# Moving part of the last scan quarter's matrix work ahead of the scan's end, and summing later output weights by DMA

## The chip, the cores and the metric

The kernel runs on one core of one Trainium2 chip, as one program. The metric is the device time of one execution in microseconds, the median over several executions. The core's engines are named as in the profile: PE (matrix multiplications, into PSUM), PEld (loading of PE's weights), DVE, ACT and POOL (elementwise work), and SP, which here only starts transfers. ACT and POOL can start transfers too; POOL's can add into their target ("accumulate").

## The reference, cut to what matters

One layer of a diffusion backbone: a bidirectional S5 mixer on 1024 latent and 256 context tokens, then a SwiGLU feed-forward network, both behind RMS norms with scale and shift. The work that the change touches is the S5 mixer:

```python
def run(u, h0):                                   # once per direction, 64 groups x 64 complex states
    bu = jnp.einsum('lgh,gnh->lgn', u, b_bar)
    bu = bu.at[0].add(lam_bar * h0)
    a = jnp.broadcast_to(lam_bar, bu.shape)
    _, h = lax.associative_scan(_linear_combine, (a, bu), axis=0)
    return jnp.einsum('lgn,ghn->lgh', h, c_mat).real, h[-1]
y = y_forward + reversed(y_backward) + d_skip * h
g = jax.nn.gelu(y);  out = g * jax.nn.sigmoid(g @ w_glu + b_glu)
```

## The kernel before, in words

The 1024 latent tokens are cut into 128 blocks of 8. Inside a block the output is a multiplication with a small lag (Toeplitz) matrix; between blocks, states are carried by a scan over 128 block positions. The 64 groups of channels are handled as four **quarters** q = 0..3, each of two **eighths** k = 2q, 2q+1. For each eighth the output is the sum of an input part (`x_mm`, L945: 16 matrix multiplications with the Toeplitz tiles) and a state part (`states_mm`, L922: the states times the quarter's output weights `CL[q]`). The state part is done in two halves, an early one over block positions whose states are there before the scan ends, and a late one; the direction that runs backwards is read through a turned copy of the states (`turned`, L902 and L904).

The scan itself (`scan`, L839 to L864) runs on DVE alone, from 128.7 to 228.57 us. It restores the odd block positions of some quarters as it goes; for others `fill` restores them on POOL, from the even ones. Everything else near it is written out by hand, in two strings of tokens: `PROG1` (L32) lists what the other engines do while the scan runs, `PROG2` (L33, L34) what follows, and `run` executes a string token by token, so a token's place fixes the order of its instructions on every engine and queue that it uses. The digit behind the letter is the eighth (for C: quarter and part, for F: quarter and half).

The tokens that matter here:

- **Cqp** (`cl_ops`, L659): part p of quarter q's output weights: two products of 128x1024 on POOL (L77) and their sum. `HOWS` (L30) says how each sum is made: P by four PE multiplications with the identity (L672) and two ACT copies (L673), E by a POOL addition (L77), Y by a transfer started by POOL that adds into its target (L675).
- **Kk** (`k_mats`): the lag matrices of an eighth: 32 + 8 + 32 PE instructions (L809, L813, L817) into two PSUM tiles that were zeroed before (`zeros`, L771, two of ACT's copies, or DVE's memset, L966), then two ACT copies (L821), each followed by a transfer to `kd` in DRAM that ACT starts (L822). **Tu** reads that back as a Toeplitz tile (SP, L830).
- **Pk**: `x_mm` and the early half of `states_mm`; **Yj**: ACT copies one of its two PSUM tiles to SBUF (L997). **Rk** turns the early states (ACT). **Nk**: the late half; **Zk** turns the late states; **Dk** adds late to early (DVE); **Hk** is the gelu (ACT).
- **Qk** (k = 6, 7 only): `x_mm` and both halves at once (`states_all`, L935), after the scan, with the gelu read from PSUM (L1009). The lag matrices K6 and K7 stand after the scan too, and so do T12 to T15.
- **I, J** transpose the result (L1056) for the gate's multiplication **g** (`glu_mm`, L1097 to L1099), which starts at 267.49 us; **w, l** load its weights, **W, V** split them for the matrix unit. After it comes the feed-forward network, to the end.

Of the kernel before, what the change touches and what calls it, by code (L numbers as in the profile page):

```python
# [42 lines left out]
def s5_ffn_kernel(tc, a, out):  # L43
# [3 lines left out]
    with ctx:  # L47
# [611 lines left out]
        def cl_ops(q, part, ct, how):  # L659
# [7 lines left out]
            def add():  # L667
# [8 lines left out]
                else:  # L676
# [18 lines left out]
        cts = [[ct_[0], ct_[0], ct_[1], ct_[2]], [ct_[0], ct_[1], ct_[2], ct_[0]], [ct_[1], ct_[2], ct_[0], ct_[1]], [ct_[3], ct_[0]] * 2]  # L695
        CL0 = cl_ops(0, 0, cts[0][0], SY) + cl_ops(0, 1, cts[0][1], SY)
        CLAT = {12: 1, 13: 1, 14: 2}
        for hb in range(16):
# [210 lines left out]
        def yview(k, gp):  # L909
            return Y[:, k].rearrange("p t (a e h) -> p e a t h", e=2, h=HC)[:, gp]  # L910

        def states_mm(k, pts, half, hs, start):

            for a_ in range(4):
                for ri in range(2):
                    for d in range(2):
                        cs_ = slice(64 * (half ^ d), 64 * (half ^ d) + 64)
                        c0 = 31 + 64 * half
                        for gp in range(2):
                            ps = slice(64 * gp, 64 * gp + 64)  # L920
                            st = hs[ps, :, ri, a_] if d else STQ[k // 2][ps, c0:c0 + 64, ri, 8 * (k % 2) + a_]
                            PE.matmul(flat(pts[gp][cs_, a_]), st, flat(CL[k // 2][ps, ri, d, 4 * (k % 2) + a_]),  # L922
                                      start=start and ri == 0, stop=ri == 1 and (start or a_ == 3))

        def states_all(k, pts, hs):

            for a_ in range(4):
                for ri in range(2):
                    for d in range(2):
                        for c in range(2):  # L930
                            cs_ = slice(64 * c, 64 * c + 64)
                            for gp in range(2):
                                ps = slice(64 * gp, 64 * gp + 64)
                                st = hs[ps, cs_, ri, a_] if d else STQ[k // 2][ps, 31 + 64 * c:95 + 64 * c, ri, 8 * (k % 2) + a_]
                                PE.matmul(flat(pts[gp][cs_, a_]), st, flat(CL[k // 2][ps, ri, d, 4 * (k % 2) + a_]),  # L935
                                          start=False, stop=a_ + ri + d == 5)
# [10 lines left out]

        scan()
        inner = {}
        HSe = [view(r, kb, [64, 2, 4]) for r, kb in ((RC[3], 14), (RC[3], 12), (RC[3], 14), (RC[3], 12), (RA, 2), (RA, 0))]  # L950
        HSl = [view(RA, STB * (i // 3) + 4.125 + 2 * (i % 3), [64, 2, 4]) for i in range(6)]
        HSq = {6: view(RA, 0, [P, 2, 4]), 7: view(RA, STB, [P, 2, 4])}

        def run(prog):


            for w in prog.split():
# [2 lines left out]
                    ada(i)  # L960
                elif op == "M":
                    mod_cols(i)
                elif op == "k":
                    KT[i] = [pe8([15 * HC]) for _ in range(2)]
                    for kv in KT[i]:
                        V.memset(kv, 0.0)  # L966
                elif op == "K":
                    k_mats(*divmod(i, 2), KT.get(i) or [kt, zeros(pw([15 * HC])) if i < 4 else pm[:, 0:15 * HC]])
                elif op == "L":
                    cs_load(i, S)  # L970
                elif op == "G":
                    cs_sign(i)
                elif op == "B":
                    bb_put(1, bb_turn(1))
                    bb_put(0, bb_turn(0))
                elif op == "C":
                    q, part = divmod(i, 10)
                    for f in cl_ops(q, part, cts[q][part], HOW[q][part]):
                        f()
                elif op == "F":  # L980
                    fill(*divmod(i, 10), *((RW, 0) if i >= 30 else (RC[3], 12)))
                elif op == "T":
                    toeplitz(i)
                elif op == "R":
                    turned(i, 0, HSe[i], S)
                elif op == "Z":
                    turned(i, 1, HSl[i], ENG[ZEN[i]])
                elif op == "z":
                    turned(i, 2, HSq[i], ENG[ZEN[i]])
                elif op == "P":  # L990
                    inner[i] = x_mm(i, pw)
                    states_mm(i, inner[i], 0, HSe[i], False)
                elif op == "Q":
                    inner[i] = x_mm(i, pe8)
                    states_all(i, inner[i], HSq[i])
                elif op == "Y":
                    S.copy(yview(i // 2, i % 2), inner[i // 2][i % 2])  # L997
                elif op == "N":
                    late[i] = [pe8([4, T, HC]) for _ in range(2)]
                    states_mm(i, late[i], 1, HSl[i], True)  # L1000
                elif op == "D":
                    for gp, po in enumerate(late[i]):
                        tt(yview(i, gp), po, yview(i, gp), ADD)
                elif op == "H":
                    if i in late:
                        S.activation(Y[:, i], Y[:, i], AF.Gelu_apprx_tanh)
                    else:
                        for gp in range(2):
                            S.activation(yview(i, gp), inner[i][gp], AF.Gelu_apprx_tanh)  # L1009
# [31 lines left out]
        KT = {}  # L1041
# [731 lines left out]
```

## Time and profile before

| what | us |
| --- | --- |
| median of 3 runs (lowest, highest) | 1023.78 (1023.33, 1025.45) |
| span of the profiled execution, first to last instruction | 1022.5 |
| scan on DVE | 128.7 to 228.57 |
| first late half (N0) on PE | 228.72 |
| first matrix multiplication of the gate | 267.49 |
| PE busy, of 25 us from 225 / from 275 | 18.78 / 25.00 |

The profiled execution has no time of its own beside its span; the median of the runs lies 1.3 us above that span, which is the time around the first and the last instruction. In rows of the timeline the first number is the start in us, the second how long the group took from its first start to its last end; what stands in brackets is how long the engine sat idle before it, and which instruction it waited for. In the rows by window, "PEclk" is the clock that PE was granted, 1.00 being full speed.

### The profile page before, as it was taken

What the parts mean: (1) busy time and instruction counts of PE and PEld (TensorE: products, weight loads), DVE (VectorE), ACT (ScalarE), POOL (GpSimd) and SP (SyncE); (2) the same over time, 40 slices, a digit from 0 to 9 for tenths busy, and PEclk for the clock granted to TensorE, in tenths of its full rate; (3) what the DMA queues carried; (4) which work ended last, traced back from release to release, by engine and by line L of the source; (5) the groups of instructions that cost most, each with busy time, mean ns of one, the idle gap of its engine ahead of it and who ended that gap; (6) DMA issues with size and microseconds to landing.
All of it is one profiled execution on the core that took longest, in us unless ns stands there. A gap on an engine that the chain in (4) does not pass through costs nothing. (4 is left out here: it accounts for less than half of the span.)

```text
span 1022.5 us, 18552 instructions
## 1 busy us (share of the span) xinstructions
PE 962.6 (94%) x6988; PEld 774.2 (76%) x6988; DVE 785.6 (77%) x1642; ACT 438.5 (43%) x858; POOL 762.7 (75%) x590
## 2 busy tenths in 40 slices
PE   5987798868999999999999999999999999999996
PEld 1466523658999988778888888888888888888885
DVE  7989799994365778788968768585958778686977
ACT  5477622324353663533334343424333343324337
POOL 5799999991591457879686877778686877777664
PEclk9999999998999999999999999999999999999998
DMA  9765997222622021011212011121212111121205
GB/s 318 292 132 96 276 350 243 91 73 57 235 80 86 2 104 62 21 42 42 83 41 73 32 52 61 43 73 52 73 42 81 41 40 56 45 70 52 72 21 165
DMA packets 48546, 98.96 MB, mean 97 GB/s; under 512 B 4284, under 2 KB 18876, under 8 KB 47176
## 3 DMA queue, kind: packets, MB, share of 16 engines
q1 hardware_dynamic: 43272, 86.64, 25.3%
q0 software_dynamic: 2016, 7.34, 3.8%
q10 hardware_dynamic: 3168, 3.79, 1.1%
q8 instruction: 55, 0.90, 0.4%
q14 instruction: 35, 0.29, 0.1%
HBM read 84.25 MB, written 6.17 MB: 88 GB/s over the span
## 5 line engine op out<-in xcount | busy, mean ns | idle before, releaser
L77 POOL TENSOR_TENSOR c<-rxc,c 128x512 fp32r<-128x512 f32 x128 | 166.6, 1316 | 53.5 <-ACT c L1227 52.7
L1287 PE MATMUL ut<-ra,c 128*128 128x512 f32 x400 | 155.7, 389 | 1.2 <-DVE ra L77 1.2
L1286 PE MATMUL ut<-ra,c 128*128 128x512 f32 x400 | 155.7, 389 | 0.2 <-ACT ra L1227 0.2
L1288 PE MATMUL ut<-ra,c 128*128 128x512 f32 x400 | 155.6, 389 | 0.0
L1227 ACT CAST c<-rxc 128x512 fp32r<-128x512 f32 x128 | 79.1, 622 | 146.8 <-PE xt L1581 53.3
L1581 PE MATMUL xt<-c,c 128*128 128x512 f32 x540 | 129.7, 389 | 0.0
L1581 PEld LDWEIGHTS xt<-c,c 128*128 128x128 f32 x540 | 101.4, 188 | 21.0
L77 DVE TENSOR_TENSOR ru<-ru,xt 128x1024 f32<-128x1024 f32 x90 | 106.8, 1213 | 8.6 <-PE xt L1581 6.6
L77 DVE TENSOR_TENSOR ru<-ut,ru 128x512 f32<-128x512 f32 x98 | 67.1, 686 | 43.1 <-PE ut L1288 37.7
L1287 PEld LDWEIGHTS ut<-ra,c 128*128 128x128 f32 x400 | 75.1, 188 | 17.1 <-POOL rxc L77 1.5
L1286 PEld LDWEIGHTS ut<-ra,c 128*128 128x128 f32 x400 | 75.1, 188 | 16.1 <-ACT ra L1227 0.6
L1288 PEld LDWEIGHTS ut<-ra,c 128*128 128x128 f32 x400 | 75.1, 188 | 15.5
L77 POOL TENSOR_TENSOR c<-rw,c 128x512 fp32r<-128x512 f32 (+1 forms) x29 | 42.5, 1465 | 38.8 <-ACT c L1227 38.2
L1286 PE MATMUL ut<-c,c 128*128 128x512 f32 x160 | 62.3, 389 | 0.8 <-DVE rxa L77 0.8
L77 POOL TENSOR_TENSOR c<-ru,c 128x512 fp32r<-128x512 f32 (+1 forms) x39 | 55.5, 1422 | 10.1 <-ACT c L1227 5.7
L77 POOL TENSOR_TENSOR rxc<-rxc 128x512 f32<-128x512 f32 x40 | 61.5, 1536 | 1.6
L1288 PE MATMUL ut<-c,c 128*128 128x512 f32 x160 | 62.3, 389 | 0.0
L1287 PE MATMUL ut<-c,c 128*128 128x512 f32 x160 | 62.3, 389 | 0.0
L1581 PE MATMUL ut<-c,c 128*128 128x512 f32 x216 | 51.9, 389 | 0.0
L584 PE MATMUL pv<-ru,c 128*64 128x160 f32 x512 | 43.7, 312 | 7.3 <-POOL ru L77 2.6
L77 DVE TENSOR_TENSOR pe<-pe,ru 128x256 f32<-128x256 f32 x64 | 27.4, 428 | 29.5 <-ACT pe L1127 17.4
L77 DVE TENSOR_TENSOR ru<-ru,ut 128x512 f32<-128x512 f32 x76 | 47.2, 678 | 0.7 <-ACT ru L1635 0.5
(449 smaller groups left out, 2576.0 us busy)
## 6 DMA issues: line engine op xcount, KB each, us to landing
c<-in_ada_w SPq DMA_DIRECT2D x46, 256.0 KB
rxc<-in_w SPq DMA_DIRECT2D x38, 256.0 KB
rxc<-in_w SPq DMA_DIRECT2D x19, 512.0 KB
ru<-in_w SPq DMA_DIRECT2D x11, 512.0 KB
rw<-in_w SPq DMA_DIRECT2D x11, 512.0 KB
ra<-in_ada_w SPq DMA_DIRECT2D x10, 512.0 KB
ra<-in_ada_w SPq DMA_DIRECT2D x18, 256.0 KB
ru<-in_xT SPq DMA_DIRECT2D x4, 1024.0 KB
```

Source lines behind the costliest of these rows:

```text
L77: eng.tensor_tensor(out=o, in0=x, in1=y, op=op)
L584: PE.matmul(pv[64 * (i % 2):64 * (i % 2) + 64, ri, c0:c0 + 160], w[:, i, 64 * ri:64 * ri + 64], U[:, 8 * b + 4 * j + i], start=True, stop= ...
L1227: S.copy(o[0], x)
L1286: PE.matmul(pu, wh, bh, start=start, stop=False)
L1287: PE.matmul(pu, wh, bl, start=False, stop=False)
L1288: PE.matmul(pu, wl, bh, start=False, stop=stop)
L1581: PE.matmul(pd, w[:, cs_], b, start=j in (1, 2, 4) and n == 0, stop=n == 2, skip_group_check=j not in (1, 2, 4))
```

## The change

Three things are changed.

1. In `HOWS`, the sums of C21, C22, C23, C30, C31 and C32 become transfers that POOL starts, and the sum of C33 becomes four PE multiplications. A fifth buffer for a second product is added (in RA), and C32 uses it.
2. The odd block positions of quarter 3 are restored one eighth at a time (`fill_k`, F6 and F7: 8 POOL instructions of 128x512) and no longer one half of the positions at a time (F30 and F31: 16 of 128x256).
3. Tokens move from `PROG2` to `PROG1`: K7 and K6, and a new early half for the eighths 6 and 7 (R6, P6, Y12, Y13, R7, P7, Y14, Y15; without `x_mm`). Q6 and Q7 become N6 and N7, `x_mm` and the late half, followed by new DVE additions D6 and D7 and one gelu each. K7 writes to the PSUM tiles of the earlier lag matrices, K6 to two new ones that ACT zeroes (L771). T12 to T15 stand at the start of `PROG2`, the first loads of the gate's weights behind H2.

```diff
-HOWS = "PPPP PPEE PEEE EEEE"
+HOWS = "PPPP PPEE PYYY YYYP"
-PROG1 = ("... C30 C31 R4 P4 Y8 Y9 C32 C33 R5 P5 Y10 Y11 M2 m0 F30 F31")
-PROG2 = ("k6 Z0 N0 Z1 Z2 D0 Z3 N1 k7 D1 Z4 H0 H1 K6 N2 D2 H2 K7 T12 T13 T14 T15 N3 Z5 D3 H3 N4 D4 z6 z7 I0 J0 I1 J1 w0 w1 l1 H4 N5 D5 I2 J2 H5 I3 J3 W0 W1 x0 x1 x2 x3"
-         " Q6 H6 I4 J4 Q7 b0 I5 J5 H7 g03 ...
+PROG1 = ("... C30 C31 R4 P4 Y8 Y9 C32 C33 R5 P5 Y10 Y11 K7 K6 M2 m0 F6 R6 P6 Y12 Y13 F7 R7 P7 Y14 Y15")
+PROG2 = ("T12 T13 T14 T15 Z0 N0 Z1 Z2 D0 Z3 N1 D1 Z4 H0 H1 N2 D2 H2 w0 w1 l1 Z6 N3 Z5 D3 H3 Z7 N4 D4 I0 J0 I1 J1 H4 N5 D5 I2 J2 H5 I3 J3 W0 W1 x0 x1 x2 x3"
+         " N6 D6 H6 I4 J4 N7 D7 b0 I5 J5 H7 g03 ...
-        ct_ = [view(r, kb, [8, T, HC]) for r, kb in ((RW, 0), (RC[3], 0), (RC[3], 4), (RA, STB))]
-        cts = [..., [ct_[3], ct_[0]] * 2]
+        ct_ = [view(r, kb, [8, T, HC]) for r, kb in ((RW, 0), (RC[3], 0), (RC[3], 4), (RA, STB), (RA, STB + 4.125))]
+        cts = [..., [ct_[3], ct_[0], ct_[4], ct_[3]]]
+        def fill_k(k):
+            tmps = [view(RA, 4.25 + 2 * i, [512]) for i in range(2)]
+            st, e = STQ[k // 2], 8 * (k % 2)
+            rot(st[:, 32:95:2, :, e:e + 8], st[:, 31:94:2, :, e:e + 8], LS[:, 0], 8 * k, E, tmps)
-                    k_mats(*divmod(i, 2), KT.get(i) or [kt, zeros(pw([15 * HC])) if i < 4 else pm[:, 0:15 * HC]])
+                    k_mats(*divmod(i, 2), [zeros(pw([15 * HC])) if i == 6 else kt, zeros(pw([15 * HC])) if i in (0, 1, 2, 3, 6) else pm[:, 0:15 * HC]])
                 elif op == "P":
-                    inner[i] = x_mm(i, pw)
-                    states_mm(i, inner[i], 0, HSe[i], False)
-                elif op == "Q":
-                    inner[i] = x_mm(i, pe8)
-                    states_all(i, inner[i], HSq[i])
+                    inner[i] = x_mm(i, pw) if i < 6 else [pw([4, T, HC]) for _ in range(2)]
+                    states_mm(i, inner[i], 0, HSe[i], i >= 6)
                 elif op == "N":
-                    late[i] = [pe8([4, T, HC]) for _ in range(2)]
-                    states_mm(i, late[i], 1, HSl[i], True)
+                    late[i] = [pe8([4, T, HC]) for _ in range(2)] if i < 6 else x_mm(i, pe8)
+                    states_mm(i, late[i], 1, HSl[i], i < 6)
```

How the change moves instructions is seen best on ACT, at the end of `PROG1`. A row names the line, the operation, output<-input and size, and the semaphores that it waits for; `pw`, `pm`, `kt` are PSUM tiles, `ra`, `ru`, `rw`, `r`, `c` SBUF regions, `kd` the lag matrices in DRAM. Before, from the turning for P5 to the first late gelu:

```order
L902 COPY ra<-ra 128x512 [waits DMAHW2_49,DMAHW1_49,DVE_49]
L997 COPY ru<-pw 128x4x8x16 [waits PE_49] x2
L902 COPY ra<-ra 128x512 [waits DVE_49]
L902 COPY ra<-ra 128x512 [waits Activation_49]
L1006 ACT_TABLE_LOAD
```

And in the change, from the copies of P5's result (Y10, Y11, L986 there) to those of P6's:

```order
L986 COPY ru<-pw 128x4x8x16 [waits PE_49] x2
L821 COPY rw<-kt 128x240 [waits DMAHW6_49,PE_49]
L822 DMA kd_1249<-rw 128x240 [waits DMAHW5_49,Activation_49]
L821 COPY rw<-pm 128x240 [waits DMAHW7_49,PE_49]
L822 DMA kd_1249<-rw 128x240 [waits Activation_49]
L771 COPY pw<-r_60 128x240 x2
L821 COPY r_60<-pw 128x240 [waits DMAHW4_49,PE_49,Activation_49]
L822 DMA kd_1249<-r_60 128x240 [waits Activation_49]
L821 COPY r_60<-pw 128x240 [waits PE_49]
L822 DMA kd_1249<-r_60 128x240 [waits DMAHW0_49,Activation_49]
L908 COPY ra<-ra 128x512 [waits Pool_49]
L986 COPY ru<-pw 128x4x8x16 [waits PE_49] x2
```

K7's copies and transfers, the two zeroings for K6, K6's copies and transfers and R6 (L908) now stand one behind another between P5's result and P6's.

On POOL, the second place: from the third part of quarter 3's weights (C32) on. Before:

```order
L77 TENSOR_TENSOR c_66<-rxc,rxa 128x1024
L77 TENSOR_TENSOR ra<-rxc,rxa 128x1024
L77 TENSOR_TENSOR c_66<-c_66,ra 128x1024 [waits Pool_49]
L77 TENSOR_TENSOR c_66<-rxc,rxa 128x1024 [waits PE_49,Activation_49]
L77 TENSOR_TENSOR rw<-rxc,rxa 128x1024
L77 TENSOR_TENSOR c_66<-c_66,rw 128x1024 [waits Pool_49]
L888 COPY r_60<-r_60 128x8
```

In the change:

```order
L77 TENSOR_TENSOR c_66<-rxc,rxa 128x1024
L77 TENSOR_TENSOR ra<-rxc,rxa 128x1024 [waits PE_49,Activation_49]
L675 DMA c_66<-ra 128x1024 [waits Pool_49]
L77 TENSOR_TENSOR c_66<-rxc,rxa 128x1024 [waits PE_49]
L77 TENSOR_TENSOR ra<-rxc,rxa 128x1024 [waits DMASW1_49]
L894 COPY r_60<-r_60 128x8
```

The additions are gone; C32's second product has a new wait for PE, and C33's for the landing of an earlier accumulating transfer.

On PE the order between P4 and N0 was P4, P5, N0; in the change it is P4, C33's four multiplications (L672), P5, K7, K6, P6, P7, N0. The first instruction of K6, and that of each direction of P6 and P7, waits for ACT or POOL there; after N0 the multiplications of K6 and K7 are gone from among the late halves.

More of the change, by code (lines that the diff above doesn't have):

```diff
@@ L29 @@
 MAGIC = 12582912.0
-HOWS = "PPPP PPEE PEEE EEEE"
+HOWS = "PPPP PPEE PYYY YYYP"
 ZEN = "VVSVSVSV"
-PROG1 = ("A22 B0 A26 C02 G1 A30 A34 C03 A40 K0 A44 A48 C10 K1 L2 A54 G2 C11 A60 F10 C12 F11 C13 T0 T1 T2 T3 A64 M0 M1 K2 R0 P0 Y0 Y1 K3 L3 R1 C20 P1 Y2 Y3 T4 T5 G3 T6 T7 C21 C22 C23 K4 R2 P2 Y4 Y5 K5 R3 P3 Y6 Y7 T8 T9 T10 T11 C30 C31 R4 P4 Y8 Y9 C32 C33 R5 P5 Y10 Y11 M2 m0 F30 F31")
-PROG2 = ("k6 Z0 N0 Z1 Z2 D0 Z3 N1 k7 D1 Z4 H0 H1 K6 N2 D2 H2 K7 T12 T13 T14 T15 N3 Z5 D3 H3 N4 D4 z6 z7 I0 J0 I1 J1 w0 w1 l1 H4 N5 D5 I2 J2 H5 I3 J3 W0 W1 x0 x1 x2 x3"
-         " Q6 H6 I4 J4 Q7 b0 I5 J5 H7 g03 g13 I6 J6 g23 g05 g15 I7 J7 V1 w20 w21 g26 x10 x11 x12 x13")
+PROG1 = ("A22 B0 A26 C02 G1 A30 A34 C03 A40 K0 A44 A48 C10 K1 L2 A54 G2 C11 A60 F10 C12 F11 C13 T0 T1 T2 T3 A64 M0 M1 K2 R0 P0 Y0 Y1 K3 L3 R1 C20 P1 Y2 Y3 T4 T5 G3 T6 T7 C21 C22 C23 K4 R2 P2 Y4 Y5 K5 R3 P3 Y6 Y7 T8 T9 T10 T11 C30 C31 R4 P4 Y8 Y9 C32 C33 R5 P5 Y10 Y11 K7 K6 M2 m0 F6 R6 P6 Y12 Y13 F7 R7 P7 Y14 Y15")
+PROG2 = ("T12 T13 T14 T15 Z0 N0 Z1 Z2 D0 Z3 N1 D1 Z4 H0 H1 N2 D2 H2 w0 w1 l1 Z6 N3 Z5 D3 H3 Z7 N4 D4 I0 J0 I1 J1 H4 N5 D5 I2 J2 H5 I3 J3 W0 W1 x0 x1 x2 x3"
+         " N6 D6 H6 I4 J4 N7 D7 b0 I5 J5 H7 g03 g13 I6 J6 g23 g05 g15 I7 J7 V1 w20 w21 g26 x10 x11 x12 x13")
 LOG2E = 1.4426950408889634
@@ L864, in scan, with fill_q @@
                 one()
-        def fill(q, h, reg, kb):
-            tmps = [view(reg, kb + i, [256]) for i in range(2)]
+        def fill_q(q, h):
+            tmps = [view(RC[3], 12 + i, [256]) for i in range(2)]
             st, c0 = STQ[q], 32 * h
@@ L910, in yview, with ypart @@
             return Y[:, k].rearrange("p t (a e h) -> p e a t h", e=2, h=HC)[:, gp]
+        def ypart(k, gp):
+            return view(RA, 2 * STB + 4.25 + 2 * gp, [4, T, HC]) if k == 7 else yview(k, gp)
         def states_mm(k, pts, half, hs, start):
@@ L923, in states_mm @@
                                       start=start and ri == 0, stop=ri == 1 and (start or a_ == 3))
[L925 to L936, printed above, removed]
         def x_mm(k, pool):
@@ L949, in s5_ffn_kernel @@
         inner = {}
-        HSe = [view(r, kb, [64, 2, 4]) for r, kb in ((RC[3], 14), (RC[3], 12), (RC[3], 14), (RC[3], 12), (RA, 2), (RA, 0))]
-        HSl = [view(RA, STB * (i // 3) + 4.125 + 2 * (i % 3), [64, 2, 4]) for i in range(6)]
-        HSq = {6: view(RA, 0, [P, 2, 4]), 7: view(RA, STB, [P, 2, 4])}
+        HSe = [view(r, kb, [64, 2, 4]) for r, kb in ((RC[3], 14), (RC[3], 12), (RC[3], 14), (RC[3], 12), (RA, 2), (RA, 0), (RA, 2), (RA, 0))]
+        HSl = [view(RA, STB * (i // 4) + 4 + 2 * (i % 4), [64, 2, 4]) for i in range(8)]
         def run(prog):
@@ L962, in run @@
                     mod_cols(i)
[L963 to L966, printed above, removed]
                 elif op == "K":
-                    k_mats(*divmod(i, 2), KT.get(i) or [kt, zeros(pw([15 * HC])) if i < 4 else pm[:, 0:15 * HC]])
+                    k_mats(*divmod(i, 2), [zeros(pw([15 * HC])) if i == 6 else kt, zeros(pw([15 * HC])) if i in (0, 1, 2, 3, 6) else pm[:, 0:15 * HC]])
                 elif op == "L":
@@ L980, in run @@
                 elif op == "F":
-                    fill(*divmod(i, 10), *((RW, 0) if i >= 30 else (RC[3], 12)))
+                    if i < 10:
+                        fill_k(i)
+                    else:
+                        fill_q(*divmod(i, 10))
                 elif op == "T":
@@ L987, in run @@
                     turned(i, 1, HSl[i], ENG[ZEN[i]])
-                elif op == "z":
-                    turned(i, 2, HSq[i], ENG[ZEN[i]])
                 elif op == "P":
-                    inner[i] = x_mm(i, pw)
-                    states_mm(i, inner[i], 0, HSe[i], False)
-                elif op == "Q":
-                    inner[i] = x_mm(i, pe8)
-                    states_all(i, inner[i], HSq[i])
+                    inner[i] = x_mm(i, pw) if i < 6 else [pw([4, T, HC]) for _ in range(2)]
+                    states_mm(i, inner[i], 0, HSe[i], i >= 6)
                 elif op == "Y":
-                    S.copy(yview(i // 2, i % 2), inner[i // 2][i % 2])
+                    S.copy(ypart(i // 2, i % 2), inner[i // 2][i % 2])
                 elif op == "N":
-                    late[i] = [pe8([4, T, HC]) for _ in range(2)]
-                    states_mm(i, late[i], 1, HSl[i], True)
+                    late[i] = [pe8([4, T, HC]) for _ in range(2)] if i < 6 else x_mm(i, pe8)
+                    states_mm(i, late[i], 1, HSl[i], i < 6)
                 elif op == "D":
                     for gp, po in enumerate(late[i]):
-                        tt(yview(i, gp), po, yview(i, gp), ADD)
+                        tt(yview(i, gp), po, ypart(i, gp), ADD)
                 elif op == "H":
[L1005 to L1009, printed above, removed]
+                    S.activation(Y[:, i], Y[:, i], AF.Gelu_apprx_tanh)
                 elif op == "I":
```

3 lines of the change are left out of this document (1 added, 2 removed).

## The prediction

> **What bounds the kernel now.** I read the busy time by window first (its columns: the window, its length, the busy time of PE, PEld, DVE, ACT and POOL with their instructions, then PE's granted clock, the DMA engines' busy share and GB/s), then PE's timeline from the last early half to the gate.
>
> ```profile
> 275.00:300.00 25.00, 25.00 (x214) 25.00 (x213) 14.69 (x33) 16.47 (x36) 23.14 (x11) 1.00 0.22 82
> 400.00:1000.00 600.00, 597.82 (x2636) 494.16 (x2635) 459.19 (x537) 227.71 (x395) 467.64 (x345) 1.00 0.16 53
> ```
>
> From 275 us PE is full, to the end (25.00 of 25, later 597.82 of 600). So what the change does to the time is what it does to the start of the gate's first multiplication, about one to one, and that start is set by PE's work after the scan:
>
> ```profile
> 219.99 1.83 PE L945 MATMUL pw<-ra,ru 128*128 128x128 f32 x14 [0.24 <-ACT ru L997]
> 221.75 2.26 PE L922 MATMUL pw<-c,ra 64*64 64x128 f32 x64
> 228.72 0.70 PE L922 MATMUL pe<-c,ra 64*64 64x128 f32 x4 [4.71 <-DVE ra L77]
> 229.77 6.44 PE L922 MATMUL pe<-c,ra 64*64 64x128 f32 x124 [0.35 <-DVE ra L904]
> 236.13 1.03 PE L809 MATMUL pe<-c,rxa 64*16 64x112 f32 x63
> 237.75 1.76 PE L922 MATMUL pe<-c,ra 64*64 64x128 f32 x46
> 240.13 1.00 PE L922 MATMUL pe<-c,ra 64*64 64x128 f32 x18 [0.62 <-issue]
> 241.06 1.03 PE L809 MATMUL pe<-c,rxa 64*16 64x112 f32 x63
> 243.58 0.41 PE L817 MATMUL pe<-rxc,rxa 64*16 64x16 f32 x34 [1.13 <-issue]
> 247.59 1.50 PE L922 MATMUL pe<-c,ra 64*64 64x128 f32 x34 [0.40 <-issue]
> 254.71 1.16 PE L945 MATMUL pe<-ra,ru 128*128 128x128 f32 x8 [0.48 <-DMA ra<-kd]
> 255.80 4.79 PE L935 MATMUL pe<-c,ra 64*64 64x128 f32 x128
> 262.89 4.26 PE L935 MATMUL pe<-c,ra 64*64 64x128 f32 x128
> 267.49 0.36 PE L1097 MATMUL pe<-c,c 128*128 128x256 f32 x1
> ```
>
> P5 ends at 224.0, PE idles 4.7 us for the scan, then N0, N1, K6, N2, K7, N3 to N5, Q6 and Q7 follow with hardly a gap up to 267.49. PE has some 5 us to spare before the scan's end and nothing after it.
>
> **What leaves PE after the scan.** K6, 236.13 to 237.75: 1.62. K7, 241.06 to about 243.92 (the end of the row at 243.58, less the overlap), with its stall of 1.13: 2.86. The stalls of 0.62 and 0.40 follow dense stretches of short K instructions and go with them; the wait of 0.48 for T12's transfer goes because that starts earlier. Q6 and Q7 keep 64 of their 128 state multiplications; 64 take 2.26 (row at 221.75), so they give 4.79 + 4.26 - 4.52 = 4.5. N0 and N1, 6.44 for 124 instructions, ran mostly at half clock; at full clock they need 2 x 2.26, which gives 2.0, if the clock is up by then. Sum: 1.62 + 2.86 + 0.62 + 0.40 + 0.48 + 4.5 + 2.0 = 12.5. The gate could begin 12.5 us earlier if N0 began when it did.
>
> **When N0 begins in the change.** Now PE must do C33's sum, K7, K6, P6 and P7 first. I follow the chain from K4, whose first need is C23's sum.
>
> ```profile
> 187.95 2.35 POOL L77 TENSOR_TENSOR c<-c,rw 128x1024 f32<-128x1024 f32 x1
> 190.26 4.02 POOL L77 TENSOR_TENSOR c<-rxc,rxa 128x1024 f32<-128x1024 f32 x2
> 196.76 0.27 PE L809 MATMUL kt<-c,rxa 64*16 64x112 f32 x1 [2.46 <-POOL c L77]
> 131.39 0.88 POOL L675 DMA_DIRECT2D c<-rw  x1 [0.30 <-POOL rw L77]
> c<-c POOLq DMA_DIRECT2D x8, 512.0 KB, 5.3
> DMA to landing us min/median/max: 7.8/8.0/8.2
> 120.00:132.00 12.00, 10.65 (x88) 3.80 (x84) 9.51 (x38) 3.09 (x7) 8.91 (x11) 0.86 1.03 340
> 185.00:195.00 10.00, 8.64 (x153) 6.00 (x141) 10.00 (x59) 3.33 (x8) 9.84 (x6) 1.00 0.43 131
> 205.49 0.36 ACT L821 COPY rw<-kt 128x240 f32<-128x240 f32 x1 [0.57 <-PE pm L817]
> 207.01 0.62 ACT L902 COPY c<-ra 128x512 f32<-128x512 f32 x1 [0.40 <-ACT rw L821]
> 208.40 3.89 SPq L830 DMA_DIRECT2D ra<-kd  x4
> 185.34 3.70 PE L672 MATMUL pw<-c,r 128*128 128x512 f32 x8
> 216.40 2.93 PE L922 MATMUL pw<-c,ra 64*64 64x128 f32 x64
> ```
>
> An addition costs POOL 2.3 (187.95 to 190.26), an accumulating transfer 0.9 at most (131.39), but it must land. C22's addition is the row at 187.95, and two products of 2.0 and C21's addition stand ahead of it, so that one began at about 181.6. With 0.9 in place of each addition and products of 2.0 (4.02 for two), C22's transfer goes out at 187.4 and C23's at about 191.5; C20's PE sum, whose buffer C23 reuses, is through by then (row at 185.34). Transfers of this size landed after 5.3 (eight of them) or 8.0 (the two of L675, before 140 us). I take 5.3, since those two ran while the DMA engines were full (share 1.03, row of 120 us) and here the share is 0.43; bounds: 1.4, the time from when ACT had sent off a small write of `kd` (207.01) to the read that waits for it (208.40), and 8.0. So C23 is there at 196.8, and K4 starts as before, at 196.76. POOL's saving of seven additions ends there: from K4 on the chain is K4, P2, K5, its `kd`, the T8 reads, P4, none of which the change touches, and P4 ends at 219.3 as before. P4's rows set what follows, not POOL: its last products wait for P3, which follows K5 (copied at 205.49) and ends some 4 us later, near 210; a product, a transfer and two products more, 2.0 + 0.9 + 4.0, and POOL is done near 217.
>
> C33's sum is new on PE: one sum took 3.54 (185.34 to the next instruction at 188.88), so P5 runs 222.9 to 226.9 (4.0, as 219.99 to 224.0). K7, in dense form, 1.62: to 228.5. Then the work goes over to ACT and back, three times:
>
> ```profile
> L771 ACT COPY pw<-r x4: 368/375/393, 149.5 to 183.3; 128x240 f32<-128x240 f32 x4
> 224.04 1.07 ACT L997 COPY ru<-pw 128x512 f32<-128x512 f32 x2 [3.09 <-PE pw L922]
> ```
>
> K7's two copies and two transfers take ACT 1.52 (205.49 to 207.01), the two zeroings 0.75: K6 waits for the zeroings, which stand behind both, until 228.6 + 1.52 + 0.75 = 230.9. This is the wait that the change adds. K6 takes 1.62 to 232.5; copies and transfers 1.52, then R6 0.62: P6 starts at about 234.9. P6 is 64 instructions, 2.26 at full clock, to 237.2. Y12 and Y13 are in front of R7 on ACT: 1.07 + 0.62, so P7 runs 238.9 to 241.2, and Y14 with a hand-over of 0.7 lets N0 begin at 241.9 (the scan has ended at 228.57, and its turned late states come behind Y15 on ACT). Against 229.77 less 4 instructions, 229.5, N0 is 12.4 later. So far 12.4 - 12.5 = -0.1: the chain gives back what the moved work saves, because PE idles about 2.4 + 2.4 + 1.7 + 0.7 = 7 us in it, and C33 adds 3.5.
>
> **The clock.** PE's clock falls after windows in which it did little (here the windows of 3.41 us with PE's busy time, its clock, the DMA share and GB/s, and from the list of PE's waits the sum, count and longest of those for the T8 reads):
>
> ```profile
> 194.28:197.69 3.41, 0.95 (x86) 1.00 0.57 173
> 197.69:201.10 3.41, 3.41 (x76) 0.50 0.32 100
> 211.33:214.75 3.42, 1.33 (x9) 1.00 0.59 149
> 214.75:218.17 3.42, 3.42 (x40) 0.50 0.32 95
> 218.17:221.58 3.41, 3.17 (x54) 1.00 0.13 49
> 228.41:231.82 3.41, 2.75 (x44) 0.50 0.00 0
> 231.82:235.23 3.41, 3.41 (x72) 0.50 0.02 5
> PE pw L945 <- DMA ra<-kd: 3.5, 2, 2.8
> ```
>
> After 0.95 and 1.33 busy of 3.4 the next window had half clock; 2.75 at half clock did not lift it, 3.42 did. In the new chain 228.41 to 231.82 holds 0.9 of K6, the next window the rest of K6, some 1.3 at half clock. So P6 falls into a slow window; at half clock 64 instructions took about 3.5 (229.77 to 235.23 at 0.50 holds about 100 of them), so +1.25. Its window then is about 3.0 busy, nearer to 2.75 than to 3.42, so P7 too is slow: +1.25. I take both: N0 14.9 later, net **+2.4**. On the profiled span this is 1024.9, and with the 1.28 by which the median lies above that span, **1026.2**. The unknown here is only the clock: 0 at the one end, and 2.0 more than +2.4 if N0 and N1 stay slow as they were.
>
> The Trainium skill, "TensorE: Matmul & The Clock Gate" (the closing rules, "Why this matters for your kernels"), asks for no PE gaps above about 3 us to keep the clock. All gaps of the new chain are shorter, so by that page the clock would hold, and the time would be 1023.7. The row of 211.33 speaks against it: its two waits were 3.5 together, the longest 2.8, and the window after it was granted 0.50. I go by the row; the full clock is a rival.
>
> **What costs nothing, and its cover.** The fills are the same elements in 8 instructions in place of 16.
>
> ```profile
> 223.02 1.41 POOL L77 TENSOR_TENSOR rw<-ra,r 128x256 f32<-128x256 f32 x2
> ```
>
> A pair took 1.41 for multiplications; at 1.5 for the additions too, an estimate from that row, the eight pairs of before take 12 and each new fill 6: from 217.6, F6 is done by 224 and F7 by 230, under K6's 232.5; without that cover R6 and R7 would wait for them. T12 to T15 go out once K6's `kd` is written, near 236, where before they stood behind K7, and the gate's first weights follow them on SP, so those come earlier too. D6 and D7 (two DVE additions each) and one gelu run beside PE, which has the gate's first 24 multiplications to do. C32's second product now waits for P3, and POOL idles for it some 2 us, under the T8 reads, for which PE itself waits 2.8.
>
> **Rivals.** (a) *The clock holds* in the new chain: net -0.1, 1023.7. For it: the windows move with the chain, and P5 with K7 fills the one before. Against it: the rows of 0.95 and 1.33.
>
> (b) *Faster: K4 no longer waits.* If C23 lands within 3.0 of its start, K4 starts up to 2.46 earlier, right behind P1; then PE is not idle in 194.28 to 197.69, P2 runs at full clock and gains 1.7 more (half of the slow window of 197.69), and everything to N0 moves by up to 4.2: +2.4 or -0.1 becomes -1.8 or -4.3; the middle is 1020.7. For it: the DMA engines are not full there. Against it: not one of the ten transfers of this size was that quick. The Trainium skill, "DMA: Bandwidth & Descriptors" (the anatomy of a POOL transfer), gives 2.0 us plus bytes by 436 GB/s, an estimate of 3.2 for these 512 KB, which is just at this point; the trace's 5.3 differs.
>
> (c) *Slower: it lands late.* At 8.0, C23 is there at 199.5, K4 starts 2.7 later, and N0 with it: +5.1, 1028.9. It decides from a landing above 5.3. For it: L675's own two took 8.0. Against it: those ran beside full DMA engines.
>
> (d) *The early halves fit before the scan's end*, the full 12.5 earlier: 1011. This needs P5 done near 216; P4's end at 219.3, set by T8, forbids it. A smaller part of it would come from hand-overs shorter than I count.
>
> **How the numbers follow.** Forecast 0.36, (a) 0.24, (b) 0.20, (c) 0.15, (d) with what else shortens the chain 0.05. This kernel's measurement tells apart about 0.2%, 2.05 us: faster is below 1021.7, slower above 1025.8. The forecast lies just above: 0.27 slower, 0.09 same. (a): 0.21 same, 0.03 faster. (b): 0.14 faster, 0.06 same. (c): slower. (d): faster. Together 0.22 faster, 0.36 same, 0.42 slower. The likeliest case's own range is 1024.5 to 1028; the one that should hold the time 8 times in 10 leaves out (d), the far end of (b) and of (c): 1019.0 to 1029.5.
>
> **What would show it.** In the changed kernel's trace: K4 still waiting until about 196.5, now for a transfer of POOL's; C33's sum on PE between P4 and P5; an idle PE before K6 with ACT's zeroing as releaser, and before P6 and P7 with ACT's turning; a clock of 0.50 in windows near 232 to 242; N0 at 242 to 245; the gate's first multiplication near 270. It is wrong if N0 begins before 238, if K4 starts by 195, or if DVE or a weight transfer holds the gate back.

## The result, and the profile after

The changed kernel took 1036.57 us (median of 4 runs, 1031.73 to 1040.31); the kernel before, beside it, 1023.56 (4 runs, 1022.24 to 1025.45). The ratio is 1.0131 with a 95% interval of 1.0109 to 1.0153: 13 us slower, where 1026.2 and a range up to 1029.5 had been forecast. The profiled execution took 1038.86, with a span of 1037.1. These 1.8 us lie around the first and the last instruction; the 1.3 of the kernel before, which the forecast used, set a median against the span of another execution, and is too small by some 0.5.

The bound is the same. PE's busy time by window, in the columns of the prediction's first rows:

```profile
275.00:300.00 25.00, 25.00 (x304) 24.52 (x304) 11.29 (x21) 12.39 (x21) 17.97 (x10) 1.00 0.54 176
400.00:1000.00 600.00, 597.80 (x2635) 494.11 (x2635) 457.62 (x537) 230.67 (x399) 472.32 (x347) 1.00 0.17 54
```

From the gate on PE is as full as before; the loss lies ahead of it. PE's timeline of the changed kernel, from K4 to the gate (L931 and L941 are the former L922 and L945, L1081 the former L1097):

```profile
204.19 0.36 PE L809 MATMUL kt<-c,rxa 64*16 64x112 f32 x1 [6.35 <-DMA c<-c]
224.66 2.04 PE L941 MATMUL pw<-ra,ru 128*128 128x128 f32 x8 [6.80 <-DMA ra<-kd]
228.77 2.07 PE L941 MATMUL pw<-ra,ru 128*128 128x128 f32 x8 [2.07 <-DMA ra<-kd]
233.61 1.12 PE L672 MATMUL pw<-c,r 128*128 128x512 f32 x2
237.15 1.95 PE L941 MATMUL pw<-ra,ru 128*128 128x128 f32 x16
239.03 2.27 PE L931 MATMUL pw<-c,ra 64*64 64x128 f32 x64
244.95 1.24 PE L809 MATMUL pw<-c,rxa 64*16 64x112 f32 x59 [2.04 <-ACT pw L771]
249.69 3.19 PE L931 MATMUL pw<-c,ra 64*64 64x128 f32 x54
254.56 2.25 PE L931 MATMUL pw<-c,ra 64*64 64x128 f32 x60 [0.52 <-ACT ra L908]
257.48 4.86 PE L931 MATMUL pe<-c,ra 64*64 64x128 f32 x147 [0.45 <-ACT ra L986]
263.78 5.72 PE L931 MATMUL pe<-c,ra 64*64 64x128 f32 x171 [1.44 <-issue]
282.64 0.36 PE L1081 MATMUL pe<-c,c 128*128 128x256 f32 x1
```

The gate begins at 282.64 in place of 267.49, 15.15 later, which is the whole of the difference between the two spans, 14.6. Stretch by stretch, each from a row above and its fellow in the prediction: K4 starts 7.43 later (204.19 against 196.76). From K4's start to P4's end it takes 29.42 and not 22.57 (233.61 and 219.33 are the ends): 6.85 more. From P4's end to P5's end it takes 7.69 and not 4.68, with C33's sum (3.54, from 233.61 to 237.15) in it: 3.01 more. From P5's end to N0's main group, 16.18 and not 5.76: 10.42 more. From there to the gate, 25.16 and not 37.72: 12.56 less. The sum is 15.15. The last two stretches, the moved work and what it saves, nearly cancel, as forecast. The first two, 14.3 us together, are the result, and the prediction had zero for both.

Where K4's delay comes from is seen on POOL, and on PE further ahead:

```profile
193.59 2.02 POOL L77 TENSOR_TENSOR c<-rxc,rxa 128x1024 f32<-128x1024 f32 x1 [4.20 <-PE pw L672]
195.91 0.87 POOL L675 DMA_DIRECT2D c<-c  x1 [0.30 <-POOL c L77]
204.23 2.01 POOL L77 TENSOR_TENSOR c<-rxc,rxa 128x1024 f32<-128x1024 f32 x1 [7.44 <-DMA c<-c]
171.15 3.15 PE L531 MATMUL pm<-c,r 128*2 128x512 f32 x7 [3.64 <-DMA c<-in_ada_w]
```

C23's sum was sent at 195.91, 4.4 later than reckoned, and was there at 204.2, 8.3 after it was sent and not 5.3. It was sent late because its second product waited 4.20 for C20's PE sum, whose buffer it takes over. PE was late with that for two reasons. The sum began at 188.12 and not at 185.34, mostly because an early load came late in this execution (3.64 of waiting at 171.15). And it took 5.2 and not 3.54: PE's granted clock was 0.51 from 188.1 to 191.0, where the profile before had 1.00.

The way from K5 to P4, on ACT and SP:

```profile
214.40 0.50 ACTq L822 DMA_DIRECT2D kd<-rw  x1
219.15 6.05 SPq L830 DMA_DIRECT2D ra<-kd  x4
```

K5's write to DRAM was sent off by 214.90, and the T8 reads that wait for it began at 219.15: 4.25, against 1.4 before (207.01 to 208.40). From the reads' start to P4's second half of `x_mm` it took 9.62 (228.77) against 6.15 (214.55). That is 2.85 + 3.47 of the 6.85. By their times, the sum beside K5's write is C31's (sent at 213.74, landed 4.8 later, 0.6 before the reads began), and the one beside the reads is C32's (sent at 220.12, landed after 8.4); C30's (sent at 208.52) had landed after 5.7, at about the time of the write.

### The profile page after: what moved, and what is told of

It is laid out like the page before. It is cut to its first block, busy times and chain, and to the rows that moved or that the text cites. A ratio compares the mean times of both kernels' runs of the same rounds, so it can differ in the third digit from the quotient of the medians.

```text
span 1037.1 us, 18589 instructions
## 1 busy us (share of the span) xinstructions
PE 968.6 (93%) x6996; PEld 776.5 (75%) x6996; DVE 783.4 (76%) x1642; ACT 443.4 (43%) x866; POOL 750.6 (72%) x581
## 5 line engine op out<-in xcount | busy, mean ns | idle before, releaser
L77 DVE TENSOR_TENSOR ru<-ut,ru 128x512 f32<-128x512 f32 x98 | 67.2, 686 | 43.1 <-PE ut L1272 37.7
L77 POOL TENSOR_TENSOR c<-rxc,rxa 128x1024 f32<-128x1024 f32 x23 | 48.4, 2183 | 11.6 <-DMA c<-c 7.4
```

The source lines that it names most:

```text
L77: eng.tensor_tensor(out=o, in0=x, in1=y, op=op)
```

## The experiments

**Theory 1** (formed on this trace): the sums by transfer cost the time. They share the DMA engines with the Toeplitz reads and the lag matrices' writes; C23's lands late, and quarter 3's hold up K5's writes and the T8 reads. **Theory 2**: the moved tokens cost it, by their waits through ACT. The first four runs put one part at a time back.

The sums alone, without the moved tokens:

```diff
 # on the kernel before
-HOWS = "PPPP PPEE PEEE EEEE"
+HOWS = "PPPP PPEE PYYY YYYP"
-        ct_ = [..., (RA, STB))]
+        ct_ = [..., (RA, STB), (RA, STB + 4.125))]
-        cts = [..., [ct_[3], ct_[0]] * 2]
+        cts = [..., [ct_[3], ct_[0], ct_[4], ct_[3]]]
```

> The kernel before with the first part of the change alone: sums by transfer and C33 on PE, with the fifth buffer; nothing is moved. Theory 1 (the transfers cost the time: C23's sum lands some 7 us late, and the sums of quarter 3 slow the way from K5 to P4 by another 7): K4 near 203, P4 ends near 230 to 234, C33's sum adds 3.5, P5 ends near 238 to 241, N0 follows at once, 9 to 12 us later than 229.77, less up to 2 for a clock that is up: 1031 to 1035. Theory 2 (the moved tokens cost the time): P5 ends by 228 and N0 is not moved: 1021 to 1026.

Measured: 1030.73 (4 runs), ratio 1.0065 (1.0042 to 1.0089) to the kernel before, whose median beside it was 1023.04.

```profile
206.58 0.36 PE L809 MATMUL kt<-c,rxa 64*16 64x112 f32 x1 [6.82 <-DMA c<-c]
226.84 2.04 PE L945 MATMUL pw<-ra,ru 128*128 128x128 f32 x8 [6.08 <-DMA ra<-kd]
242.12 4.45 PE L922 MATMUL pe<-c,ra 64*64 64x128 f32 x128 [1.16 <-ACT ru L997]
```

K4 and P4 wait for transfers as in the changed kernel, and N0 starts at 242.12 with nothing moved ahead of it. This is theory 1, a little below its numbers. The gate begins at 276.67 in this profile, 9.2 later than before.

The moved tokens alone, with the old row of sums:

```diff
 # on the changed kernel
-HOWS = "PPPP PPEE PYYY YYYP"
+HOWS = "PPPP PPEE PEEE EEEE"
```

> The changed kernel with the old row of sums (C21 to C23 and C30 to C33 added on POOL); the tokens stay moved. Theory 1: K4 and P4 as before (196.8, end 219.3), P5 ends at 224.0, from there 16 us to N0 as in the changed kernel's trace, N0 near 240, then 25.1 to the gate: gate near 265, 1020 to 1023. Theory 2: the gate stays more than 8 us late, 1032 or more.

Measured: 1020.91 (10 runs), ratio 0.9978 (0.9960 to 0.9996).

```profile
213.03 1.13 PE L941 MATMUL pw<-ra,ru 128*128 128x128 f32 x8 [2.75 <-DMA ra<-kd]
222.04 2.28 PE L931 MATMUL pw<-c,ra 64*64 64x128 f32 x64
232.76 3.70 PE L931 MATMUL pw<-c,ra 64*64 64x128 f32 x62 [1.08 <-ACT ra L908]
238.13 3.48 PE L931 MATMUL pw<-c,ra 64*64 64x128 f32 x58 [0.32 <-ACT ra L908]
241.49 5.21 PE L931 MATMUL pe<-c,ra 64*64 64x128 f32 x154
266.57 0.36 PE L1081 MATMUL pe<-c,c 128*128 128x256 f32 x1
```

P4 waits for T8 as before (2.75), P5 ends at 224.3, N0 starts 17.2 later, the gate at 266.57. Theory 2 falls: the moved tokens gain 2 us.

Quarter 2's sums on POOL again, quarter 3's left as transfers:

```diff
 # on the changed kernel
-HOWS = "PPPP PPEE PYYY YYYP"
+HOWS = "PPPP PPEE PEEE YYYP"
```

> The changed kernel with quarter 2's sums on POOL again; quarter 3's stay transfers. Splits theory 1. If C23's landing before K4 is all of it: K4 near 197, P4 ends near 220, P5 near 227, N0 near 243: 1022 to 1026. If quarter 3's sums slow the lag matrices' transfers by 7 as well: P4 ends near 226, 1029 to 1031.

Measured: 1030.30 (4 runs), ratio 1.0065 (1.0042 to 1.0087).

And the other way round, quarter 2's as transfers and quarter 3's on POOL:

```diff
 # on the changed kernel
-HOWS = "PPPP PPEE PYYY YYYP"
+HOWS = "PPPP PPEE PYYY EEEE"
```

> The changed kernel with quarter 3's four sums on POOL; quarter 2's stay transfers. If C23's landing alone counts: K4 near 203, P4 ends near 226, P5 near 230 (no C33 on PE), N0 near 246: 1027 to 1029. If quarter 3's transfers are the larger part: K4 to P4 takes 22.5 us as before, and the time is that of K4's delay alone, 1023 to 1028, below the run with quarter 2 on POOL.

Measured: 1024.93 (10 runs, 1019.92 to 1032.56), ratio 1.0023 (1.0000 to 1.0045). The timelines, first of the run with quarter 3's transfers, then of the one with quarter 2's:

```profile
214.91 1.41 PE L941 MATMUL pw<-ra,ru 128*128 128x128 f32 x5 [6.11 <-DMA ra<-kd]
```

```profile
191.89 0.87 POOL L675 DMA_DIRECT2D c<-c  x1 [0.30 <-POOL c L77]
200.05 0.37 PE L809 MATMUL kt<-c,rxa 64*16 64x112 f32 x1 [6.97 <-DMA c<-c]
216.14 1.17 PE L941 MATMUL pw<-ra,ru 128*128 128x128 f32 x8 [3.09 <-DMA ra<-kd]
```

Quarter 3's transfers double P4's wait (6.11 against 2.75); quarter 2's make K4 wait (6.97, for a sum sent at 191.89) and leave P4's alone (3.09). So both halves of theory 1 hold. By the medians quarter 3's sums cost 9.4 us over the moved tokens alone and quarter 2's 4.0; both cost 15.7 (1036.57 less 1020.91). Each of these differences is uncertain by some 2 to 3 us, as the intervals of the ratios say. On the kernel before, the same sums cost only 7.7 (1030.73 less 1023.04). There P5 ended 17.0 later (at 241.0), but N0's main group began only 12.4 later, since PE's 4.7 us of idle time ahead of N0 took up part of the delay; the moved tokens fill that time.

Why a landing takes 8 us was tried by leaving out the reads that run beside it:

```diff
 # on the run with quarter 2 by transfer and quarter 3 on POOL
-PROG1 = ("... P1 Y2 Y3 T4 T5 G3 T6 T7 C21 ...
+PROG1 = ("... P1 Y2 Y3 G3 C21 ...
```

> Quarter 2's sums by transfer, quarter 3's on POOL, tokens moved, and the four Toeplitz reads T4 to T7 left out, so that P2 and P3 multiply by the tiles of T0 to T3 (that part of the result is not computed). In the run with those reads C23's sum was sent at 191.89 and K4 could start at 200.05, 8.2 later. If the landing is slow because T4 to T7 share the DMA engines with it: the landing falls to 4.7 to 5.5 us and K4 starts at 196.5 to 197.5. If an accumulating transfer of this buffer needs 8 us by itself: no change, 200.

Measured: 1025.76 (one run). The answer is in the lists of transfers, where the last number of a row is the time to landing. In the run with the reads, C21's sum, C22's, two of the reads and C23's sum:

```profile
c<-c POOLq DMA_DIRECT2D x1, 512.0 KB, 4.7
c<-rw POOLq DMA_DIRECT2D x1, 512.0 KB, 7.8
ra<-kd SPq DMA_DIRECT2D x2, 256.0 KB
c<-c POOLq DMA_DIRECT2D x1, 512.0 KB, 8.1
```

Without them, C23's sum in that list:

```profile
c<-c POOLq DMA_DIRECT2D x1, 512.0 KB, 5.0
```

And in the timeline of the run without them:

```profile
192.46 0.87 POOL L675 DMA_DIRECT2D c<-c  x1 [0.30 <-POOL c L77]
197.48 0.27 PE L809 MATMUL kt<-c,rxa 64*16 64x112 f32 x1 [4.10 <-DMA c<-c]
```

With T4 to T7 beside it C23's sum takes 8.1, without them 5.0, and K4 starts at 197.5 in place of 200.05. The 5.3 of the prediction is near the price of such a sum that runs nearly alone. C22's sum stays at 7.5 without the reads (7.8 with them), so it was slowed by something else. A load of 512 KB (G3, `rxc<-in_cxy`) went out 0.8 us ahead of it there, and 0.9 ahead in the run with the reads; in the change, where that load went out 3.6 behind it, C22's sum took 5.2. That the load does it was not tried. The time of this one run, 1025.76, is not below the other's 1024.93; a single execution can't show K4's 2.6 us in the total.

Which of quarter 3's sums matter, with C32's alone as a transfer:

```diff
 # on the moved tokens alone
-HOWS = "PPPP PPEE PEEE EEEE"
+HOWS = "PPPP PPEE PEEE EEYP"
```

> Tokens moved; of all the sums in question only C32's is a transfer (it is sent after the T8 reads have begun to land) and C33's is made on PE; the others are added on POOL. If it is the transfers of C30 and C31, beside K5's writes to DRAM and the T8 reads, that hold P4 back: K4 to P4's end takes 22.5 us as before, P4 ends near 219.5, P5 3.5 later than without C33 on PE, near 227.5, the gate near 268 to 270, 1023 to 1026. If any transfer of quarter 3 has that effect: P4 ends after 221.5 and the time is that of the run with all three, about 1030.

Measured: 1026.37 (10 runs), ratio 1.0025 (1.0014 to 1.0037). P4's wait for T8 is as without transfers:

```profile
213.64 1.44 PE L941 MATMUL pw<-ra,ru 128*128 128x128 f32 x8 [2.98 <-DMA ra<-kd]
```

This clears C32's transfer only where it stands here: it went out at 214.59, when P4 had its first T8 tile already, and in the change it went out 1 us behind the start of the reads. The time was 5.5 above the moved tokens alone, though, and this led to the two last runs, which take C33's PE sum and the transfers apart:

```diff
 # on the moved tokens alone; first run, then second
-HOWS = "PPPP PPEE PEEE EEEE"
+HOWS = "PPPP PPEE PEEE EEEP"
+HOWS = "PPPP PPEE PEEE YYYE"
```

> Tokens moved, all sums on POOL but C33's, which PE makes between P4 and P5. If that sum lies fully on the path: P5 ends 3.5 later than with POOL's addition, near 227.8, and the time is 3.5 above the run with the moved tokens alone (1020.9): 1023.5 to 1025.5. If PE had room for it: 1021 to 1022.

Measured: 1026.28 (7 runs), ratio 1.0030 (1.0018 to 1.0042), the kernel before having 1022.98 beside it.

```profile
220.81 1.42 PE L672 MATMUL pw<-c,r 128*128 128x512 f32 x2
226.52 2.28 PE L931 MATMUL pw<-c,ra 64*64 64x128 f32 x64
236.69 2.26 PE L931 MATMUL pw<-c,ra 64*64 64x128 f32 x62 [1.29 <-ACT ra L908]
250.52 6.04 PE L931 MATMUL pe<-c,ra 64*64 64x128 f32 x171 [2.13 <-issue]
269.71 0.36 PE L1081 MATMUL pe<-c,c 128*128 128x256 f32 x1
```

One sum on PE costs 5.4 us by the medians, some 2 us either way. P5 ends 4.5 later than with the moved tokens alone (228.8 against 224.3), of which 3.8 is the sum (from 220.81 to the next `x_mm` at 224.64). The two profiles don't show the whole 5.4: their gates are 3.1 apart. From P5's end to N0 it takes 2.5 less here (14.7 against 17.2), because P6 and P7 run at full clock (62 instructions in 2.26, against 3.70 there), and from N0 to the gate 1.1 more, of which 0.9 is the stall (2.13 here, 1.25 there). C32's transfer at its place in the run before adds nothing that can be told apart (1026.37 against 1026.28).

> Tokens moved, quarter 2's sums on POOL, C30 to C32 as transfers, C33 added on POOL. The run with C33 on PE as well gave 1030.3. If the transfers beside K5's writes and the T8 reads cost some 2 to 6 and C33 on PE 3.5: 1024 to 1028, with K4 to P4's end 25 to 28 us. If PE's sum is free: 1030 again.

Measured: 1028.11 (4 runs), ratio 1.0054 (1.0033 to 1.0076).

```profile
195.79 0.27 PE L809 MATMUL kt<-c,rxa 64*16 64x112 f32 x1 [3.04 <-POOL c L77]
211.46 0.87 POOL L675 DMA_DIRECT2D c<-ra  x1 [0.30 <-POOL ra L77]
218.22 2.04 PE L941 MATMUL pw<-ra,ru 128*128 128x128 f32 x8 [9.03 <-DMA ra<-kd]
223.39 2.66 PE L931 MATMUL pw<-c,ra 64*64 64x128 f32 x64
```

Here P4 waits 9.03, and K4 to P4's end takes 30.3, without any PE sum: the transfers of C30 to C32 cost 7.2 over the moved tokens. Which of the three does it is not separated: C32's went out at 211.46 here, when the T8 reads had just begun (at 211.29). So both parts of quarter 3's row cost, 5.4 and 7.2; together they cost 9.4 (1030.30), less than their sum of 12.6, which the uncertainty of 2 to 3 us in each allows.

Two runs were on the moved tokens themselves. One zeroes K6's PSUM tiles earlier:

```diff
 # on the moved tokens alone
-PROG1 = ("... R5 P5 Y10 Y11 K7 K6 M2 ...
+PROG1 = ("... R5 P5 Y10 k6 Y11 K7 K6 M2 ...
 ...
+                elif op == "k":
+                    KT[i] = [zeros(pw([15 * HC])) for _ in range(2)]
```

> Tokens moved, sums on POOL as before, and K6's two PSUM tiles zeroed ahead of K7's copies. If the wait of K6 for the zeroing (2.04 us of idle PE in the run without this) is on the path: P6, P7 and N0 move up by about 2, and the time is 1.5 to 2.5 below that run. If POOL's fills set P6 and P7 (F6 ended at 228.0, F7 at 233.3 there, and R7 was done at 238.1): less, P7 is then held by R6 and R7 on ACT, 0 to 1.5.

Measured: 1022.95 (10 runs), ratio 0.9993 (0.9980 to 1.0007): no gain; the 2 us that it lies above 1020.91 are within the two intervals.

```profile
226.58 0.97 PE L809 MATMUL pw<-c,rxa 64*16 64x112 f32 x45
229.26 0.46 PE L809 MATMUL pw<-c,rxa 64*16 64x112 f32 x18 [1.71 <-issue]
232.73 3.70 PE L931 MATMUL pw<-c,ra 64*64 64x128 f32 x62 [1.12 <-ACT ra L908]
```

K6 begins at once, and then stalls 1.71 in its own issue, so that its result is there at the same time as before and P6 starts at 232.73 against 232.76. The wait for the zeroing was on the path, and another of its size stood behind it.

The other moves K7 and K6 alone, on the kernel before, with K6's tiles zeroed early and the transfers that hang on them (T12 to T15 and the gate's first weights) moved up; it leaves everything else of the change out:

```diff
 # on the kernel before
-PROG1 = ("... R5 P5 Y10 Y11 M2 m0 F30 F31")
+PROG1 = ("... R5 P5 Y10 k6 Y11 K7 K6 M2 m0 F30 F31")
-PROG2 = ("k6 Z0 N0 Z1 Z2 D0 Z3 N1 k7 D1 Z4 H0 H1 K6 N2 D2 H2 K7 T12 T13 T14 T15 N3 Z5 D3 H3 N4 D4 z6 z7 I0 J0 I1 J1 w0 w1 l1 H4 ...
+PROG2 = ("T12 T13 T14 T15 Z0 N0 Z1 Z2 D0 Z3 N1 D1 Z4 H0 H1 N2 D2 H2 w0 w1 l1 N3 Z5 D3 H3 N4 D4 z6 z7 I0 J0 I1 J1 H4 ...
-                    KT[i] = [pe8([15 * HC]) for _ in range(2)]
-                    for kv in KT[i]:
-                        V.memset(kv, 0.0)
+                    KT[i] = [zeros(pw([15 * HC])) for _ in range(2)]
```

> The kernel before with K7 and K6 alone moved ahead of the scan's end (K6's tiles zeroed early), T12 to T15 and the gate's first weights moved up; sums on POOL, fills, Q6 and Q7 as before, no early halves. PE has 4.7 us free there and K7 and K6 need 3.2, so N0 should begin at 228.7 as before, and K6, K7, their stalls and the wait for T12 leave the path: 1.62 + 2.86 + 0.48 = 5.0, and up to 2.0 more if PE's clock stays up over N0 and N1, up to 1.0 if the other stalls go: 1016 to 1019. If the hand-overs through ACT delay N0 as they did in the change: no gain, 1022 to 1025.

Measured: 1016.16 (6 runs), ratio 0.9930 (0.9911 to 0.9949), against 1022.86 beside it: 7 us faster than the kernel before, and faster than every other run.

```profile
226.49 2.27 PE L922 MATMUL pw<-c,ra 64*64 64x128 f32 x64
232.69 0.46 PE L809 MATMUL pw<-c,rxa 64*16 64x112 f32 x18 [1.51 <-issue]
233.80 12.60 PE L922 MATMUL pe<-c,ra 64*64 64x128 f32 x320
263.51 0.36 PE L1095 MATMUL pe<-c,c 128*128 128x256 f32 x1
```

In this execution the scan ended 3.3 us later than in the profile before (at 231.88), and P5 4.8 later (228.8 for 224.0). K7 and K6 still nearly fit into the time that PE had to wait: N0's main group begins 1.9 behind the scan's end, 1.2 in the profile before. N0 to N4 then run in one piece, 320 instructions in 12.60 without a stall, and from 233.80 it takes 29.7 to the gate and not 37.7.

The runs' places beside each other, in us, from the same rows of each trace:

| run | K4 starts | K4 to P4's end | P5 ends | N0 (main group) | gate | median |
| --- | --- | --- | --- | --- | --- | --- |
| before | 196.8 | 22.6 | 224.0 | 229.8 | 267.5 | 1023.0 |
| sums and C33 alone, nothing moved | 206.6 | 26.7 | 241.0 | 242.1 | 276.7 | 1030.7 |
| moved tokens alone | 196.8 | 22.8 | 224.3 | 241.5 | 266.6 | 1020.9 |
| + C33 on PE | 197.2 | 23.6 | 228.8 | 243.5 | 269.7 | 1026.3 |
| + C30 to C32 by transfer, C33 on POOL | 195.8 | 30.3 | 230.8 | 245.4 | 270.3 | 1028.1 |
| + C30 to C32 by transfer, C33 on PE | 195.8 | 25.3 | 228.8 | 245.1 | 272.8 | 1030.3 |
| + C21 to C23 by transfer | 200.1 | 23.6 | 228.4 | 242.3 | 267.2 | 1024.9 |
| the change | 204.2 | 29.4 | 241.3 | 257.5 | 282.6 | 1036.6 |
| K7 and K6 alone | 200.1 | 24.0 | 228.8 | 233.8 | 263.5 | 1016.2 |

One profiled execution of a kernel can stand some us from its median, so the last column, and not the gate's, is what a part costs.

## Why the prediction was wrong

**The step that failed** is "So C23 is there at 196.8, and K4 starts as before", and with it "from K4 on the chain is K4, P2, K5, its `kd`, the T8 reads, P4, none of which the change touches, and P4 ends at 219.3 as before". Three things were wrong in it.

*The landing's price.* I had two rows, 5.3 and 8.0, and chose the lower by the DMA engines' share, 0.43 from 185 to 195 us; most of that window lies ahead of the sending, which I put at 191.5. In the landing itself the T4 to T7 reads stand (sent from 193.84 to 197.88 in the changed kernel, C23's sum at 195.91); with them it took 8.1 to 8.7, without them 5.0. It was rival (c), with its price right for K4 (2.7 to 3) and too small in all, since it ended at K4.

*The cover of the buffer.* I wrote that C20's PE sum "is through by then". By my own times it was by 0.5 us (188.88, against 189.4 for the second product's start), which is less than an early load varies by; in the changed kernel's profile POOL waited 4.20 for it. With the sums alone it waited 2.68, behind a load that was late too (3.82), and in the run with quarter 2's transfers, where the load came in time, not at all. So part of K4's 7.4 is the chance of that execution; the landing's part is 3.0 to 3.3. In the kernel before there was no such wait, since the additions kept POOL behind PE.

*The chain that "the change doesn't touch".* No instruction of it is touched; its transfers are. Quarter 3's sums run beside K5's writes and the T8 reads, the writes could be read 2.85 later, and the reads took 3.47 longer. The runs put the three transfers together at 7.2 us, some 3 either way. No rival had it: I asked of each transfer when it lands, and not what it does to the ones beside it.

**What held.** The moved work was sized right. P5's end to N0 was forecast as 15.0 at full clock and 17.5 with P6 and P7 slow: 16.2 in the change, with P6 slow (54 instructions in 3.19 at 249.69) and P7 not (60 in 2.25 at 254.56), 17.2 in the run with the moved tokens alone, with both slow (3.70 and 3.48), and 13.9 to 14.8 in the four runs in which both ran at full speed (those with C32 alone by transfer, with C33 on PE, with quarter 2's transfers, and with C30 to C32 by transfer and C33 on POOL). So both prices were right, but "I take both" was not a reading that holds for this chain: the clock in it differs between runs whose waits are nearly the same. K6 waited 2.04 to 2.13 and P6 1.08 to 1.29 in all of these. The clock was 0.50 from 229.9 to 241.8 in the profile of the moved tokens alone, and 1.00 from 225 to 247 in that with C33 on PE. The Trainium skill, "TensorE: Matmul & The Clock Gate" (closing rules), asks for no PE gaps above about 3 us to keep the clock. No wait in that stretch was longer than 2.2 in these runs, so by that page all of them would have kept the clock; three did (C32 alone by transfer, C33 on PE, quarter 2's transfers), and in the change and the moved tokens alone it fell to 0.50 all the same. Rival (a) is open in that sense; what decides it was not tried.

The wait of K6 behind K7's copies and the zeroing stands there as forecast (2.04). N0 to the gate was forecast as 25.2 and took 25.2, though not by the terms given: the stalls of 0.62 and 0.40 did not go with the K instructions, since one of 1.25 to 2.57 stands in the late halves of every run that has them in one dense block with P6 and P7 ahead (1.44 in the change); the dense block's instructions were a little faster than the 2.26 for 64 that I used (318 in 4.86 + 5.72), which gave part of it back. C33's sum took the 3.54 that it was given, but cost 5.4. In sum the forecast of +2.4 less C33 is a forecast of about -1 for the moved tokens alone, which measured -2.1. That the whole change is slower, as forecast, is luck: the forecast had +2.4 from the moved work and C33, and the slowdown came from two stretches that it put at zero.

**Rival (b)**, an early landing, and **rival (d)** are excluded: the shortest landing measured among the sums in question, 4.6, is far from the 3.0 that (b) needed, and P4 never ended before 219. The estimate of 3.2 from the Trainium skill, "DMA: Bandwidth & Descriptors" (the anatomy of a POOL transfer), is below every landing seen here.

**What stays open.** K4 to P4's end took 25.3, 26.7, 29.4 and 30.3 in the four runs with quarter 3's transfers; what sets the size each time was not taken apart, nor which of the three transfers holds up what. In three of these runs the T8 reads began 4.0 to 5.1 after K5's last write had been sent, each time 0.5 to 0.9 after C31's sum had landed; in the fourth (the changed kernel with quarter 2's sums back on POOL) they began after 1.44, as without a sum, though C31's was in flight. Nor was it tried how much of the change's spread, 8.6 us over 4 runs against some 5 of the kernel before over 23, comes from the early load. The cause of the stalls was not tried either.

## What to carry to other kernels

Replacing an engine's additions by accumulating transfers saves that engine's time, but the sum is there only when the transfer has landed, and that took longer where other transfers were in flight. Look up which transfers of the critical chain are in flight in the same microseconds, and price the new one with them beside it, and them with it. An engine's saved time is worth nothing where the next step waits for the landing, and a unit that was late all the time can be what kept a buffer's reuse from waiting.

When a package of edits nearly cancels on paper, run its parts: here moving two small blocks of matrix work into a wait that PE had anyway gave 7 us, and the rest of the package cost 20.

## What the runs showed of the hardware

- An accumulating transfer of 512 KB landed after 4.6 to 5.7 us at most places between 180 and 216 us, and after 7.0 to 8.7 where four reads of 256 KB were in flight; taking those reads away brought one of them from 8.1 to 5.0.
- A write of 120 KB that was read back after 1.4 us needed 4.0 to 5.1 beside such a sum in three runs, and 1.44 in a fourth.
- PE was granted half clock where no wait was longer than 2.1 us: P6 took 3.70 for 62 instructions behind waits of 2.04 and 1.08. In other runs, behind waits of 2.04 and 1.29, the same 62 took 2.26.
- Dense stretches of small matrix multiplications stalled for 0.4 to 2.6 us with nothing that they waited for in the trace. Removing a wait ahead of K6 brought such a stall up in its place (1.71 where 2.04 had been waited).
